# MoE gate and dispatch: tokens laid out as contiguous runs per partition, with large chunks and no transpose

## The chip, the cores and the metric

The kernel runs on one core of a Trainium2 chip. The metric is the device time of one execution in microseconds (us). Before the change it is 252.4 us, the median of 4 runs (252.34 to 252.94). A profiled execution of the same kernel gives the page and the trace; its span, from the first to the last instruction, is 250.4 us.

## What is computed

For each of 16 x 1024 = 16,384 tokens, the two largest of 8 router probabilities are found and normalized to a sum of one. The output holds the token's 512 numbers twice, once for each of the two gates, multiplied by that gate. The lower gate comes first.

```python
x             = randn(16, 1024, 512)   # float32
router_logits = randn(16, 1024, 8)     # float32
k = 2

logits_max = np.max(router_logits, axis=-1, keepdims=True)
probs = np.exp(router_logits - logits_max)
probs = probs / np.sum(probs, axis=-1, keepdims=True)
topk_indices = np.argsort(probs, axis=-1)[..., -k:]
topk_probs = np.take_along_axis(probs, topk_indices, axis=-1)
topk_probs = topk_probs / np.sum(topk_probs, axis=-1, keepdims=True)
x_expanded = x[:, :, np.newaxis, :].repeat(k, axis=2)
return (x_expanded * topk_probs[..., np.newaxis]).astype(np.float32)
```

With k = 2 the normalized gates are the sigmoid of the difference of the two largest logits, and the sigmoid of its negative. The input x is 33.55 MB, the logits are 0.52 MB, and the output is 67.11 MB.

## The kernel before

The 16,384 tokens are seen as 128 tiles of 128 tokens. Token `n*128 + p` lies in tile `n` on partition `p`. One tile of x is 128 rows of 2 KB that lie side by side in memory, and one tile of the output is 128 rows of 4 KB, also side by side.

```python
x_t = x_f.rearrange("(n p) d -> p n d", p=P)
o_t = o_f.rearrange("(n p) d -> p n d", p=P)
rl_A = rl_f.rearrange("(j q) e -> j (q e)", j=P)
...
GRP = 1
NGRP = NT // GRP
xbufs = ctx.enter_context(tc.tile_pool(name="xbufs", bufs=20))
obufs = ctx.enter_context(tc.tile_pool(name="obufs", bufs=8))

logitsA = wpool.tile([P, NT, E], mybir.dt.float32)
nc.sync.dma_start(logitsA, rl_A.rearrange("p (q e) -> p q e", e=E))
```

The logits are loaded in another layout: partition `j` holds those of the 128 neighbouring tokens of tile `j`. On them VectorE finds the two maxima with four wide operations (a maximum, a comparison, a masking, a maximum) and subtracts them. The difference then stands with tiles on partitions, while the scaling needs it with tokens on partitions, so TensorE transposes it through an identity matrix, and ScalarE makes the two sigmoids out of PSUM.

```python
dA = wpool.tile([P, NT], mybir.dt.float32)
nc.vector.tensor_tensor(dA, V[:, :, 0], V[:, :, 1], op=subtract)
dB = psum.tile([P, P], mybir.dt.float32)
nc.tensor.transpose(dB, dA, identity)
nc.scalar.activation(WB[:, 1, :], dB, Sigmoid, scale=1.0)
nc.scalar.activation(WB[:, 0, :], dB, Sigmoid, scale=-1.0)
```

The main loop handles one tile at a time: a load of 256 KB on SyncE's queue, two scalings on VectorE, and a store of 512 KB on ScalarE's queue.

```python
for g in range(NGRP):                       # 128 times
    xg = xbufs.tile([P, GRP, D], f32, tag="xg")
    nc.sync.dma_start(xg, x_t[:, g*GRP:(g+1)*GRP, :])
    og = obufs.tile([P, GRP, K*D], f32, tag="og")
    for slot in range(K):                   # jj loop of one pass left out
        nc.vector.tensor_scalar_mul(
            og[:, 0, slot*D:(slot+1)*D], xg[:, 0, :], WB[:, slot, g:g+1])
    nc.scalar.dma_start(o_t[:, g*GRP:(g+1)*GRP, :], og)
```

There are 20 buffers for tiles of x and 8 for tiles of the output.

Of the kernel before, what the change touches and what calls it, by code (L numbers as in the profile page):

```python
# [1 line left out]

# [5 lines left out]


@with_exitstack
def kernel(
    ctx: ExitStack,
    tc: tile.TileContext,
    x: bass.AP,
    router_logits: bass.AP,
    k: bass.AP,
    out: bass.AP,
):
    nc = tc.nc  # L20
    P = 128

    B, S, D = x.shape
    E = router_logits.shape[-1]
    K = int(k)
    N = B * S

    assert N % P == 0
    NT = N // P
    assert NT == 128, "kernel currently specialised to 16384 tokens"  # L30
    assert E <= 64
    assert 2 <= K <= E

    x_f = x.rearrange("b s d -> (b s) d")
    o_f = out.rearrange("b s k d -> (b s) (k d)")
    rl_f = router_logits.rearrange("b s e -> (b s) e")

    x_t = x_f.rearrange("(n p) d -> p n d", p=P)
    o_t = o_f.rearrange("(n p) d -> p n d", p=P)

    rl_A = rl_f.rearrange("(j q) e -> j (q e)", j=P)

    const = ctx.enter_context(tc.tile_pool(name="const", bufs=1))
    wpool = ctx.enter_context(tc.tile_pool(name="wpool", bufs=1))
    psum = ctx.enter_context(tc.tile_pool(name="psum", bufs=1, space=bass.MemoryType.PSUM))

    GRP = 1
    NGRP = NT // GRP
    xbufs = ctx.enter_context(tc.tile_pool(name="xbufs", bufs=20))
    obufs = ctx.enter_context(tc.tile_pool(name="obufs", bufs=8))  # L50

    logitsA = wpool.tile([P, NT, E], mybir.dt.float32)
    nc.sync.dma_start(logitsA, rl_A.rearrange("p (q e) -> p q e", e=E))  # L53

    identity = const.tile([P, P], mybir.dt.float32)
    make_identity(nc, identity)

    V = wpool.tile([P, NT, K], mybir.dt.float32)
    cur = logitsA
    for i in range(K):  # L60
        nc.vector.reduce_max(  # L61
            V[:, :, i : i + 1], cur, axis=mybir.AxisListType.X
        )
        if i < K - 1:
            eq = wpool.tile([P, NT, E], mybir.dt.float32, tag=f"eq{i}")
            nxt = wpool.tile([P, NT, E], mybir.dt.float32, tag=f"nxt{i}")
            nc.vector.tensor_tensor(  # L67
                eq, cur, V[:, :, i : i + 1].to_broadcast([P, NT, E]),
                op=mybir.AluOpType.is_ge,
            )  # L70
            nc.vector.scalar_tensor_tensor(  # L71
                nxt, eq, -1.0e30, cur,
                op0=mybir.AluOpType.mult, op1=mybir.AluOpType.add,
            )
            cur = nxt

    WB = const.tile([P, K, P], mybir.dt.float32)
    if K == 2:
        dA = wpool.tile([P, NT], mybir.dt.float32)
        nc.vector.tensor_tensor(dA, V[:, :, 0], V[:, :, 1],  # L80
                                op=mybir.AluOpType.subtract)
        dB = psum.tile([P, P], mybir.dt.float32)
        nc.tensor.transpose(dB, dA, identity)  # L83
        nc.scalar.activation(WB[:, 1, :], dB,  # L84
                             mybir.ActivationFunctionType.Sigmoid, scale=1.0)
        nc.scalar.activation(WB[:, 0, :], dB,  # L86
                             mybir.ActivationFunctionType.Sigmoid, scale=-1.0)
    else:
        Em = wpool.tile([P, NT, K], mybir.dt.float32)
        nc.vector.tensor_tensor(  # L90
            Em, V, V[:, :, 0:1].to_broadcast([P, NT, K]),
            op=mybir.AluOpType.subtract,
        )
        nc.scalar.activation(Em, Em, mybir.ActivationFunctionType.Exp)
        Ssum = wpool.tile([P, NT], mybir.dt.float32)
        nc.vector.reduce_sum(Ssum, Em, axis=mybir.AxisListType.X)
        Rinv = wpool.tile([P, NT], mybir.dt.float32)
        nc.vector.reciprocal(Rinv, Ssum)
        W = wpool.tile([P, NT, K], mybir.dt.float32)
        nc.vector.tensor_tensor(  # L100
            W, Em, Rinv.to_broadcast([P, NT, K]), op=mybir.AluOpType.mult
        )
        WB_ps = psum.tile([P, K, P], mybir.dt.float32)
        for slot in range(K):
            nc.tensor.transpose(WB_ps[:, slot, :], W[:, :, K - 1 - slot], identity)
        nc.vector.tensor_copy(WB, WB_ps)

    for g in range(NGRP):
        xg = xbufs.tile([P, GRP, D], mybir.dt.float32, tag="xg")
        nc.sync.dma_start(xg, x_t[:, g * GRP : (g + 1) * GRP, :])  # L110
        og = obufs.tile([P, GRP, K * D], mybir.dt.float32, tag="og")
        for jj in range(GRP):
            j = g * GRP + jj
            for slot in range(K):
                nc.vector.tensor_scalar_mul(  # L115
                    og[:, jj, slot * D : (slot + 1) * D],
                    xg[:, jj, :],
                    WB[:, slot, j : j + 1],
                )
        nc.scalar.dma_start(o_t[:, g * GRP : (g + 1) * GRP, :], og)  # L120


# [1 line left out]
_INS = ['x', 'router_logits', 'k']  # L124
_OUTS = [((16, 1024, 2, 512), 'float32')]
#: Inputs that are plain numbers.
_NUMBERS = {'k': 2}


# [26 lines left out]
```

## Time and profile before

| | before |
|---|---|
| time, median of 4 | 252.4 us |
| span of the profiled execution | 250.4 us |
| bytes moved | 101.26 MB (34.08 read, 67.11 written) |
| mean rate over the span | 404 GB/s |
| VectorE busy | 117.4 us (47%) |
| scaling operations | 256, mean 483 ns |
| loads of x | 128 of 256 KB, median 7.0 us from issue to landing |
| stores | 128 of 512 KB, median 7.5 us from issue to landing |
| first scaling starts | 10.2 us |

In the profile, PE is TensorE's matmul, PEld its weight load, DVE VectorE, ACT ScalarE, POOL GpSimd, SP SyncE; q1 is the DMA queue that SyncE issues to and q10 the one that ScalarE issues to. A row of 40 digits cuts the span in 40 equal slices of 6.3 us, and each digit is the busy share in tenths. The GB/s row has the bytes moved in the same slices. The chain of work that ended last is followed back from the last instruction, and its shares tell which engine or transfer the end hung on. A row of the groups reads: line, engine, operation, output and inputs, shape and count, then busy time in us and mean ns of one, then the idle time of the engine just before these instructions and what ended most of it. A row of the stages reads: the stretch and its length in us; for PE, PEld, DVE, ACT and POOL the busy us and the number of instructions; the granted clock of TensorE; the DMA engines' mean busy share; and GB/s. Shares of DMA can exceed 1 a little where packets of one engine overlap.

### The profile page before, as it was taken

What the parts mean: (1) busy time and instruction counts of PE and PEld (TensorE: products, weight loads), DVE (VectorE), ACT (ScalarE), POOL (GpSimd) and SP (SyncE); (2) the same over time, 40 slices, a digit from 0 to 9 for tenths busy, and PEclk for the clock granted to TensorE, in tenths of its full rate; (3) what the DMA queues carried; (4) which work ended last, traced back from release to release, by engine and by line L of the source; (5) the groups of instructions that cost most, each with busy time, mean ns of one, the idle gap of its engine ahead of it and who ended that gap; (6) DMA issues with size and microseconds to landing.
All of it is one profiled execution on the core that took longest, in us unless ns stands there. A gap on an engine that the chain in (4) does not pass through costs nothing.

```text
span 250.4 us, 932 instructions
## 1 busy us (share of the span) xinstructions
PE 0.4 (0%) x1; PEld 0.2 (0%) x1; DVE 117.4 (47%) x261; ACT 1.7 (1%) x3; POOL 0.7 (0%) x6
## 2 busy tenths in 40 slices
PE   0000000000000000000000000000000000000000
PEld 0000000000000000000000000000000000000000
DVE  3874334344454454454443544544544454467720
ACT  2000000000000000000000000000000000000000
POOL 1000000000000000000000000000000000000000
DMA  7999999999999999999999999999999999999995
GB/s 235 385 411 408 416 410 415 410 418 416 412 417 413 417 414 415 414 417 416 413 417 413 415 416 415 416 415 416 415 414 416 414 415 415 415 419 416 416 414 214
DMA packets 37015, 101.26 MB, mean 404 GB/s; under 512 B 4112, under 2 KB 4112, under 8 KB 37008
## 3 DMA queue, kind: packets, MB, share of 16 engines
q10 hardware_dynamic: 18432, 67.12, 65.6%
q1 hardware_dynamic: 18576, 34.09, 35.7%
q14 instruction: 7, 0.06, 0.1%
HBM read 34.08 MB, written 67.11 MB: 404 GB/s over the span
## 4 chain that ended last, share of the span: by engine, by line
DMA 91%; SPq 2%; DVE 2%; issue 1%; DVEq 0%; ACTq 0%
DMA out_dram<-og 83%; DMA xg<-in_x_dram 8%; SPq L110 2%; DVE og L115 2%; DVEq L151 0%; ACTq L120 0%; SPq L53 0%; DVEq L115 0%
## 5 line engine op out<-in xcount | busy, mean ns | idle before, releaser
L115 DVE TENSOR_SCALAR og<-xg,WB 128x512 f32<-128x512 f32 x256 | 112.2, 483 | 119.0 <-DMA out_dram<-og 78.2
L61 DVE TENSOR_REDUCE V<-logitsA 128x128 f32<-128x1024 f32 x1 | 1.2, 1220 | 3.9 <-DMA logitsA<-in_router_logits_dram 3.9
L84 ACT ACT_TABLE_LOAD x1 | 1.3, 1283 | 0.7 <-PEq L137 0.7
L67 DVE TENSOR_TENSOR eq<-logitsA,V 128x1024 f32<-128x1024 f32 x1 | 1.2, 1226 | 0.0
L71 DVE SCALAR_TENSOR_TENSOR nxt<-eq,logitsA 128x1024 f32<-128x1024 f32 x1 | 1.2, 1224 | 0.0
L61 DVE TENSOR_REDUCE V<-nxt 128x128 f32<-128x1024 f32 x1 | 1.2, 1220 | 0.0
L83 PE MATMUL dB<-identity,dA 128*128 128x128 f32 x1 | 0.4, 446 | 9.4 <-DVE dA L80 9.4
L84 ACT ACTIVATE WB<-dB 128x128 f32<-128x128 f32 x1 | 0.3, 277 | 7.9 <-PE dB L83 7.9
L80 DVE TENSOR_TENSOR dA<-V 128x128 f32<-128x128 f32 x1 | 0.3, 291 | 0.0
masks.py:199 POOL TENSOR_SCALAR_AFFINE_SELECT identity<-identity 128x128 f32<-128x128 f32 x1 | 0.3, 292 | 0.1
L86 ACT ACTIVATE WB<-dB 128x128 f32<-128x128 f32 x1 | 0.3, 272 | 0.0
masks.py:197 POOL MEMSET identity<- 128x128 f32 x1 | 0.2, 204 | 0.3 <-POOLq L137 0.3
L83 PEld LDWEIGHTS dB<-identity,dA 128*128 128x128 f32 x1 | 0.2, 184 | 9.4 <-issue 9.4
L137 POOL MEMSET const-bfloat16-1.0<- 128x1 bf16 x1 | 0.1, 101 | 0.0
L137 POOL MEMSET const-uint8-127<- 128x1 uint8 x1 | 0.1, 101 | 0.0
L137 POOL MEMSET const-float32-0.0<- 128x1 f32 x1 | 0.1, 98 | 0.2 <-issue 0.2
L137 POOL MEMSET const-float32-1.0<- 128x1 f32 x1 | 0.1, 98 | 0.0
## 6 DMA issues: line engine op xcount, KB each, us to landing
out_dram<-og ACTq DMA_DIRECT2D x128, 512.0 KB, 7.5
xg<-in_x_dram SPq DMA_DIRECT2D x128, 256.0 KB, 7.0
logitsA<-in_router_logits_dram SPq DMA_DIRECT2D x1, 512.0 KB, 3.2
```

What stands on the lines that cost most here:

```text
L61: nc.vector.reduce_max(V[:, :, i : i + 1], cur, axis=mybir.AxisListType.X)
L67: nc.vector.tensor_tensor(eq, cur, V[:, :, i : i + 1].to_broadcast([P, NT, E]), op=mybir.AluOpType.is_ge,)
L71: nc.vector.scalar_tensor_tensor(nxt, eq, -1.0e30, cur, op0=mybir.AluOpType.mult, op1=mybir.AluOpType.add,)
L80: nc.vector.tensor_tensor(dA, V[:, :, 0], V[:, :, 1], op=mybir.AluOpType.subtract)
L83: nc.tensor.transpose(dB, dA, identity)
L84: nc.scalar.activation(WB[:, 1, :], dB, mybir.ActivationFunctionType.Sigmoid, scale=1.0)
L86: nc.scalar.activation(WB[:, 0, :], dB, mybir.ActivationFunctionType.Sigmoid, scale=-1.0)
L110: nc.sync.dma_start(xg, x_t[:, g * GRP : (g + 1) * GRP, :])
L115: nc.vector.tensor_scalar_mul(og[:, jj, slot * D : (slot + 1) * D], xg[:, jj, :], WB[:, slot, j : j + 1],)
L137: nc = _bacc.Bacc("TRN2", target_bir_lowering=False, num_devices=1)
```

## The change

Tokens are assigned to partitions the other way round: partition `p` holds the 128 neighbouring tokens `p*128` to `p*128 + 127`. The logits are in this layout already, so the gates come out where the scaling needs them, and the transpose, the identity and PSUM are gone. A load and a store now take 8 tokens of each partition at once: 16 KB runs in x (2 MB in all) and 32 KB runs in the output (4 MB). Between the runs of neighbouring partitions lie 256 KB in x and 512 KB in the output. There are 16 chunks, and 2 buffers for each of x and the output. The first chunk is stored in four parts of 1, 1, 2 and 4 tokens per partition, so that stores begin earlier. The purpose is longer runs in memory, fewer transfers and a shorter way to the gates.

```diff
-    x_t = x_f.rearrange("(n p) d -> p n d", p=P)
-    o_t = o_f.rearrange("(n p) d -> p n d", p=P)
+    x_v = x.rearrange("b s d -> (b s) d").rearrange("(p m) d -> p m d", p=P)
+    o_v = out.rearrange("b s k d -> (b s) (k d)").rearrange(
+        "(p m) d -> p m d", p=P
+    )
...
-    GRP = 1
-    NGRP = NT // GRP
-    xbufs = ctx.enter_context(tc.tile_pool(name="xbufs", bufs=20))
-    obufs = ctx.enter_context(tc.tile_pool(name="obufs", bufs=8))
+    L = 8
+    NCH = M // L
+    xbufs = ctx.enter_context(tc.tile_pool(name="xbufs", bufs=2))
+    obufs = ctx.enter_context(tc.tile_pool(name="obufs", bufs=2))
...
-    identity = const.tile([P, P], mybir.dt.float32)
-    make_identity(nc, identity)
...
-        dB = psum.tile([P, P], mybir.dt.float32)
-        nc.tensor.transpose(dB, dA, identity)
-        nc.scalar.activation(WB[:, 1, :], dB,
-                             mybir.ActivationFunctionType.Sigmoid, scale=1.0)
+        nc.scalar.activation(
+            WA[:, 1, :], dlt, mybir.ActivationFunctionType.Sigmoid, scale=1.0
+        )
...
-    for g in range(NGRP):
-        xg = xbufs.tile([P, GRP, D], mybir.dt.float32, tag="xg")
-        nc.sync.dma_start(xg, x_t[:, g * GRP : (g + 1) * GRP, :])
+    for c in range(NCH):
+        xg = xbufs.tile([P, L, D], mybir.dt.float32, tag="xg")
+        nc.sync.dma_start(xg, x_v[:, c * L : (c + 1) * L, :])
+        og = obufs.tile([P, L, K * D], mybir.dt.float32, tag="og")
+        for l in range(L):
+            m = c * L + l
             for slot in range(K):
                 nc.vector.tensor_scalar_mul(
-                    og[:, jj, slot * D : (slot + 1) * D],
-                    xg[:, jj, :],
-                    WB[:, slot, j : j + 1],
+                    og[:, l, slot * D : (slot + 1) * D],
+                    xg[:, l, :],
+                    WA[:, slot, m : m + 1],
                 )
-        nc.scalar.dma_start(o_t[:, g * GRP : (g + 1) * GRP, :], og)
+            if c == 0 and l in (0, 1, 3):  # first chunk: stores of 1, 1, 2, 4 tokens
+                lo = (0, 1, None, 2)[l]
+                nc.scalar.dma_start(o_v[:, lo : l + 1, :], og[:, lo : l + 1, :])
+        lo = 4 if c == 0 else 0
+        nc.scalar.dma_start(o_v[:, c * L + lo : (c + 1) * L, :], og[:, lo:L, :])
```

More of the change, by code (lines that the diff above doesn't have):

```diff
@@ L6 @@
 from concourse import bass_utils, mybir
-from concourse.masks import make_identity
 from concourse._compat import with_exitstack
@@ L28 @@
     assert N % P == 0
-    NT = N // P
-    assert NT == 128, "kernel currently specialised to 16384 tokens"
+    M = N // P
     assert E <= 64
     assert 2 <= K <= E
-    x_f = x.rearrange("b s d -> (b s) d")
-    o_f = out.rearrange("b s k d -> (b s) (k d)")
-    rl_f = router_logits.rearrange("b s e -> (b s) e")
-    x_t = x_f.rearrange("(n p) d -> p n d", p=P)
-    o_t = o_f.rearrange("(n p) d -> p n d", p=P)
-    rl_A = rl_f.rearrange("(j q) e -> j (q e)", j=P)
-    const = ctx.enter_context(tc.tile_pool(name="const", bufs=1))
@@ L44 @@
-    wpool = ctx.enter_context(tc.tile_pool(name="wpool", bufs=1))
-    psum = ctx.enter_context(tc.tile_pool(name="psum", bufs=1, space=bass.MemoryType.PSUM))
-    GRP = 1
-    NGRP = NT // GRP
-    xbufs = ctx.enter_context(tc.tile_pool(name="xbufs", bufs=20))
-    obufs = ctx.enter_context(tc.tile_pool(name="obufs", bufs=8))
-    logitsA = wpool.tile([P, NT, E], mybir.dt.float32)
-    nc.sync.dma_start(logitsA, rl_A.rearrange("p (q e) -> p q e", e=E))
-    identity = const.tile([P, P], mybir.dt.float32)
@@ L56 @@
-    make_identity(nc, identity)
-    V = wpool.tile([P, NT, K], mybir.dt.float32)
-    cur = logitsA
+    x_v = x.rearrange("b s d -> (b s) d").rearrange("(p m) d -> p m d", p=P)
+    o_v = out.rearrange("b s k d -> (b s) (k d)").rearrange(
+        "(p m) d -> p m d", p=P
+    )
+    rl_v = router_logits.rearrange("b s e -> (b s) e").rearrange(
+        "(p m) e -> p m e", p=P
+    )
+    wpool = ctx.enter_context(tc.tile_pool(name="wpool", bufs=1))
+    L = 8
+    assert M % L == 0
+    NCH = M // L
@@ L60 @@
+    xbufs = ctx.enter_context(tc.tile_pool(name="xbufs", bufs=2))
+    obufs = ctx.enter_context(tc.tile_pool(name="obufs", bufs=2))
+    logits = wpool.tile([P, M, E], mybir.dt.float32)
+    nc.sync.dma_start(logits, rl_v)
+    V = wpool.tile([P, M, K], mybir.dt.float32)
+    cur = logits
     for i in range(K):
-        nc.vector.reduce_max(
-            V[:, :, i : i + 1], cur, axis=mybir.AxisListType.X
-        )
+        nc.vector.reduce_max(V[:, :, i : i + 1], cur, axis=mybir.AxisListType.X)
@@ L64 @@
         if i < K - 1:
-            eq = wpool.tile([P, NT, E], mybir.dt.float32, tag=f"eq{i}")
-            nxt = wpool.tile([P, NT, E], mybir.dt.float32, tag=f"nxt{i}")
+            eq = wpool.tile([P, M, E], mybir.dt.float32, tag=f"eq{i}")
+            nxt = wpool.tile([P, M, E], mybir.dt.float32, tag=f"nxt{i}")
             nc.vector.tensor_tensor(
-                eq, cur, V[:, :, i : i + 1].to_broadcast([P, NT, E]),
+                eq, cur, V[:, :, i : i + 1].to_broadcast([P, M, E]),
                 op=mybir.AluOpType.is_ge,
@@ L75 @@
             cur = nxt
-    WB = const.tile([P, K, P], mybir.dt.float32)
+    WA = wpool.tile([P, K, M], mybir.dt.float32)
     if K == 2:
-        dA = wpool.tile([P, NT], mybir.dt.float32)
-        nc.vector.tensor_tensor(dA, V[:, :, 0], V[:, :, 1],
-                                op=mybir.AluOpType.subtract)
-        dB = psum.tile([P, P], mybir.dt.float32)
-        nc.tensor.transpose(dB, dA, identity)
-        nc.scalar.activation(WB[:, 1, :], dB,
-                             mybir.ActivationFunctionType.Sigmoid, scale=1.0)
-        nc.scalar.activation(WB[:, 0, :], dB,
-                             mybir.ActivationFunctionType.Sigmoid, scale=-1.0)
+        dlt = wpool.tile([P, M], mybir.dt.float32)
+        nc.vector.tensor_tensor(
+            dlt, V[:, :, 0], V[:, :, 1], op=mybir.AluOpType.subtract
+        )
+        nc.scalar.activation(
+            WA[:, 1, :], dlt, mybir.ActivationFunctionType.Sigmoid, scale=1.0
+        )
+        nc.scalar.activation(
+            WA[:, 0, :], dlt, mybir.ActivationFunctionType.Sigmoid, scale=-1.0
+        )
     else:
-        Em = wpool.tile([P, NT, K], mybir.dt.float32)
+        Em = wpool.tile([P, M, K], mybir.dt.float32)
         nc.vector.tensor_tensor(
-            Em, V, V[:, :, 0:1].to_broadcast([P, NT, K]),
+            Em, V, V[:, :, 0:1].to_broadcast([P, M, K]),
             op=mybir.AluOpType.subtract,
@@ L94 @@
         nc.scalar.activation(Em, Em, mybir.ActivationFunctionType.Exp)
-        Ssum = wpool.tile([P, NT], mybir.dt.float32)
+        Ssum = wpool.tile([P, M], mybir.dt.float32)
         nc.vector.reduce_sum(Ssum, Em, axis=mybir.AxisListType.X)
-        Rinv = wpool.tile([P, NT], mybir.dt.float32)
+        Rinv = wpool.tile([P, M], mybir.dt.float32)
         nc.vector.reciprocal(Rinv, Ssum)
[L99 to L103, printed above, removed]
-        for slot in range(K):
-            nc.tensor.transpose(WB_ps[:, slot, :], W[:, :, K - 1 - slot], identity)
-        nc.vector.tensor_copy(WB, WB_ps)
-    for g in range(NGRP):
-        xg = xbufs.tile([P, GRP, D], mybir.dt.float32, tag="xg")
-        nc.sync.dma_start(xg, x_t[:, g * GRP : (g + 1) * GRP, :])
-        og = obufs.tile([P, GRP, K * D], mybir.dt.float32, tag="og")
-        for jj in range(GRP):
-            j = g * GRP + jj
+        for slot in range(K):
+            nc.vector.tensor_tensor(
+                WA[:, slot, :],
+                Em[:, :, K - 1 - slot],
+                Rinv,
+                op=mybir.AluOpType.mult,
+            )
+    for c in range(NCH):
[4 more added lines that the diff above has]
+            m = c * L + l
             for slot in range(K):
                 nc.vector.tensor_scalar_mul(
-                    og[:, jj, slot * D : (slot + 1) * D],
-                    xg[:, jj, :],
-                    WB[:, slot, j : j + 1],
-                )
-        nc.scalar.dma_start(o_t[:, g * GRP : (g + 1) * GRP, :], og)
+                    og[:, l, slot * D : (slot + 1) * D],
+                    xg[:, l, :],
+                    WA[:, slot, m : m + 1],
+                )
+            if c == 0 and l in (0, 1, 3):
[3 more added lines that the diff above has]
+        nc.scalar.dma_start(o_v[:, c * L + lo : (c + 1) * L, :], og[:, lo:L, :])
 _INS = ['x', 'router_logits', 'k']
```

## The prediction

> **What bounds the kernel now.** I read the page from the top: first the busy times, then the 40 slices, then the queues, the chain, and last the trace cut into stages. The first two say which resource is full.
>
> ```profile
> PE 0.4 (0%) x1; PEld 0.2 (0%) x1; DVE 117.4 (47%) x261; ACT 1.7 (1%) x3; POOL 0.7 (0%) x6
> ...
> DMA  7999999999999999999999999999999999999995
> GB/s 235 385 411 408 416 410 415 410 418 416 412 417 413 417 414 415 414 417 416 413 417 413 415 416 415 416 415 416 415 414 416 414 415 415 415 419 416 416 414 214
> ```
>
> No engine is more than half busy; the DMA row is 9 in every slice but the first and last, and the bytes flow at 410 to 419 GB/s from slice 3 to slice 39. The chain agrees: it is nearly all transfers, and VectorE's own work is 2% of it.
>
> ```profile
> DMA 91%; SPq 2%; DVE 2%; issue 1%; DVEq 0%; ACTq 0%
> ...
> L115 DVE TENSOR_SCALAR og<-xg,WB 128x512 f32<-128x512 f32 x256 | 112.2, 483 | 119.0 <-DMA out_dram<-og 78.2
> ```
>
> VectorE's 119.0 us of idle time before the scaling line is mostly a wait for a store to give its buffer back (78.2 us). That is how a DMA-bound loop looks from the engine, and removing engine work can't shorten it. So the span is bytes over rate, plus a start and an end. The stages give these two:
>
> ```profile
> 0.00:2.00 2.00, 0.00 (x0) 0.00 (x0) 0.00 (x0) 1.27 (x1) 0.70 (x6) 1.00 0.14 41
> ...
> 4.00:6.00 2.00, 0.00 (x0) 0.00 (x0) 1.97 (x2) 0.00 (x0) 0.00 (x0) 1.00 0.93 285
> ...
> 8.00:10.00 2.00, 0.45 (x1) 0.18 (x1) 1.23 (x2) 0.11 (x1) 0.00 (x0) 1.00 1.04 396
> ...
> 100.00:200.00 100.00, 0.00 (x0) 0.00 (x0) 45.88 (x104) 0.00 (x0) 0.00 (x0) 1.00 1.04 415
> ...
> 240.00:244.00 4.00, 0.00 (x0) 0.00 (x0) 0.46 (x2) 0.00 (x0) 0.00 (x0) 1.00 1.03 415
> ```
>
> The last two columns are the DMA engines' busy share and GB/s. 101.26 MB at 415 GB/s are 244.0 us. The span is 250.4 us, so 6.4 us lie outside the plateau: about 2.0 us until bytes flow, about 1.5 us lost to slow transfers between 2 and 9 us, and about 2.9 us from the last full-rate stretch (near 247.5 us) to the end. The reported time is 2.0 us above the span (252.4 against 250.4).
>
> The queue lines show in what pieces the bytes move:
>
> ```profile
> DMA packets 37015, 101.26 MB, mean 404 GB/s; under 512 B 4112, under 2 KB 4112, under 8 KB 37008
> ...
> q10 hardware_dynamic: 18432, 67.12, 65.6%
> q1 hardware_dynamic: 18576, 34.09, 35.7%
> ```
>
> 18,432 packets over 128 stores are 144 each: 128 of data, one row of 4 KB per partition, and 16 short ones, one per DMA engine. The loads have the same count with 2 KB rows. So every piece is 2 or 4 KB.
>
> **What the Trainium skill says.** Three places, all in "DMA: Bandwidth & Descriptors". (1) "Where 436 GB/s comes from": 16 ports give a ceiling of 435 GB/s. The plateau of 415 is 95% of that; no run so far shows 435. (2) "Why small descriptors are slow (HBM only)": every packet carries a fixed overhead of a few cycles, so larger pieces lose less; "Measured" on the same page has 425 GB/s for a 16 MB load. The trace fits an overhead: in steady state (60 to 200 us) the store queue held 67.6% of 16 engines and moved 38.71 MB, the load queue held 35.9% and moved 19.33 MB. Per data packet, with its share of the short ones, that is 0.160 us for 4 KB and 0.085 us for 2 KB. The shares add up to 1.036, because packets overlap, so I divide by that: 154.6 and 82.2 ns. The second 2 KB cost 72.4 ns, so some 10 ns of each packet don't depend on its size. (3) "Latency and other measured facts", the row on HBM row pitch: copies with a pitch of 512 KiB between partitions ran at 207 GB/s per direction against 214 when padded, larger powers of two at far less. No trace here shows such a pitch yet: before, the 128 rows of a transfer lie side by side.
>
> **The change part by part.**
>
> *Gates.* The transpose goes: matmul 0.45 us, its hand-over to ScalarE, and the identity on GpSimd, which was never on the path. The four wide VectorE operations (1.2 us each) and the subtract stay. Before, the gates were ready at about 10.2 us; without PE they could be ready at about 9.8. But the first x chunk is now 2.10 MB and VectorE needs all of it. The trace before had moved about 2.9 MB by 10 us, and logits plus chunk 0 are 2.62 MB, so with completion the chunk arrives at about 10 to 11 us. The 0.4 us are hidden. Gain: 0.
>
> *VectorE.* 256 scalings at 483 ns stay: 16 of them, 7.7 us, for each of 16 chunks. A chunk moves 2.10 MB in and 4.19 MB out, 14 to 15 us of transfer. When a chunk's scaling starts, a 4.19 MB store has just been queued or is still running, about 10 us of work, so DMA stays fed with only two buffers of each kind. Cost in steady state: 0, but the margin is about 2 us against issue and completion times.
>
> *Start.* Loads queued ahead shrink from 20 tiles (5.2 MB) to two chunks (4.2 MB), which last until about 13 to 14 us. Stores then start with one token of every partition (0.52 MB), at about 11 us issued and 12.5 us flowing, and follow at the rate of VectorE: 0.52 MB per 0.97 us. The fourth store of the first chunk (2.1 MB) must wait for four tokens, 3.9 us, while the 1.05 MB before it last only 2.5 us; load 2 also comes only when chunk 0 is finished. I put 1.0 us of idle DMA here.
>
> *End.* The last chunk is scaled in 7.7 us beside the store of the one before (9.8 us at 430 GB/s), which just covers it with issue and completion. I put 0.5 us.
>
> *Rate.* This is where any gain must come from. A load now has 16 KB runs per partition and a store 32 KB (4 to 16 KB in the first chunk), and there are 36 transfers instead of 257. If a run moves as one piece, the overhead of 10 ns per piece nearly vanishes: 72.4 ns per 2 KB alone would be 453 GB/s, above the skill's ceiling, so the ceiling would bind: about 432 GB/s. If the hardware cuts runs into pieces of 4 KB, loads and stores both look like the stores of before: 154.6 ns for 4 KB, 424 GB/s at most; but the store-only end of the trace, all 4 KB rows, shows just 415, so I say 416 to 421. If the pitch costs something (512 KiB between output rows, 256 KiB between input rows) the 3% of the skill's row would take 432 to about 419.
>
> *Sum.* Fixed parts: 6.4 us as before, plus 1.5 us, is 7.9 us; plus 2.0 us from span to time. With 432 GB/s: 234.4 + 7.9 + 2.0 = 244.3 us. With 428: 236.6 + 9.9 = 246.5 us. With 420: 241.1 + 9.9 = 251.0 us. With 415: 253.9 us.
>
> **The rivals.**
>
> *A: long runs, ceiling reached (430 to 434 GB/s), 243 to 246 us.* For it: the fixed part per packet in the trace, and that the logits transfer already moves a merged 4 KB run per partition although its view has rows of 32 bytes (18,576 packets on q1 are 129 transfers of 144). Against: store-only stages don't exceed 420 now.
>
> *B: the plateau isn't set by packets but by HBM, or runs are cut up; 415 to 422 GB/s, 250 to 254 us.* For it: the store-only end (4 KB) runs at 415, the mixture of 2 and 4 KB at 415 too, and loads of 2 KB alone at 396 to 410 around 10 us. If packet size were everything, the stores alone ought to be visibly faster than the mixture. Then only the 1.5 us of new idle time would be seen.
>
> *C: the pitch collides.* All 16 engines write at addresses that differ by multiples of 512 KiB; if that costs 5% or more, the rate falls to 395 to 405, 260 to 266 us. Against it: the skill's figure at 512 KiB is only 3% low, [...]and a third of the bytes has half the pitch.
>
> *D: two buffers are too few.* If issue plus completion takes over 2 us on top of 7.7 us, DMA idles in each of 14 chunks by perhaps 0.5 us: 7 us, which would eat A's gain. Against it: a load and a store are queued together, so there are usually two transfers outstanding.
>
> **Range and chances.** I take A as somewhat likelier than B, and lean the point to 428 GB/s: 246.5 us. Faster by 2% means under 247.4 us, a rate of at least 426.5 GB/s: 0.47. Within 2% (247.4 to 257.4 us) is B, or A spoiled by D or a mild C: 0.41. Slower is C or a bad D: 0.12. The range of 241.5 to 253.0 us holds A and most of B.
>
> **What would show it.** If A is right, the packet list has data packets over 8 KB (128 per transfer, some 4,100 in all), and plateau slices near 430 GB/s with a DMA share of 9. Packets still under 8 KB, some 25,000 of them, with 416 to 422 GB/s, mean B. A busy share of 9 with under 410 GB/s means C. Slices with a share of 7 or 8, and VectorE waiting while the queues are short, mean D. The start is right if the first scaling begins at 10 to 11 us; the end, if full rate holds to about 3 us before the end. I am wrong outright if the plateau leaves 395 to 434 GB/s, or if start and end lose over 5 us more than before.

## The result and the profile after

The changed kernel takes 242.66 us in the median (before, in runs beside it: 252.53 us). The ratio is 0.9621, with a 95% interval of 0.9598 to 0.9644: 3.8% faster. The prediction had said 246.5 us, in a range of 241.5 to 253.0.

The first lines are from the changed kernel's page: busy times, packets, queues, the chain by engine, and the group of the scaling line.

```profile
DVE 107.9 (44%) x261; ACT 1.8 (1%) x3; POOL 0.2 (0%) x4
...
DMA packets 5186, 101.21 MB, mean 415 GB/s; under 512 B 576, under 2 KB 576, under 8 KB 960
...
q10 hardware_dynamic: 2736, 67.11, 65.7%
q1 hardware_dynamic: 2448, 34.08, 33.0%
...
DMA 68%; DVE 26%; issue 0%; DVEq 0%; ACT 0%
...
L106 DVE TENSOR_SCALAR og<-xg,WA 128x512 f32<-128x512 f32 x256 | 102.7, 481 | 118.3 <-DMA out_dram<-og 118.0
```

The bytes are the same, but 5,186 packets carry them where 37,015 did. On q10, 19 stores of 128 rows and 16 short packets each make the 2,736: so a run of 32 KB goes as one packet and is not cut. VectorE still waits for stores (118.0 us), so the kernel is still bound by DMA. The 26% of the chain on VectorE are no new bound: a chunk's scaling must end before its store can start, but other transfers run beside it (the DMA row below is 9 in every slice but the first and last).

That execution was a disturbed one (span 244.1 us; the ratios leave such runs out, the medians do not), so the rates are read from a second profile of the same kernel, with a span of 240.1 us. Its 40 slices:

```profile
DMA  6999999999999999999999999999999999999995
GB/s 262 437 401 426 434 431 445 434 408 404 456 437 412 439 431 439 420 423 461 404 442 445 418 439 431 433 423 426 458 420 426 439 428 418 423 461 415 437 437 235
```

And its stages; the columns are as before, without PE and PEld, as TensorE does nothing now:

```profile
4.00:6.00 2.00, 1.54 (x2) 0.00 (x0) 0.00 (x0) 1.00 0.94 401
...
12.00:14.00 2.00, 2.00 (x6) 0.00 (x0) 0.00 (x0) 1.00 0.88 336
...
60.00:200.00 140.00, 63.53 (x159) 0.00 (x0) 0.00 (x0) 1.00 1.01 432
...
215.00:220.00 5.00, 0.00 (x0) 0.00 (x0) 0.00 (x0) 1.00 0.95 410
```

The engines were full before (share 1.04) and are full now (1.01), yet they move 432 GB/s instead of 415. The slices swing more, from 404 to 461 in the steady part, presumably because a packet of 16 or 32 KB is counted in one lump; the 401 of the third slice is a real dip (the row for 12 to 14 us). 101.21 MB at 432 GB/s are 234.3 us against 244.0 us, 9.7 us less. What lies outside the plateau is 5.8 us (240.1 - 234.3) against 6.4 us. Both together are the 10.3 us between the spans.

### The profile page after: what moved, and what is told of

Its sections match the earlier page's. It is cut to its first block, busy times and chain, and to the rows that moved or that the text cites. A ratio compares the mean times of both kernels' runs of the same rounds, so it can differ in the third digit from the quotient of the medians.

```text
span 244.1 us, 392 instructions
## 1 busy us (share of the span) xinstructions
DVE 107.9 (44%) x261; ACT 1.8 (1%) x3; POOL 0.2 (0%) x4
## 2 busy tenths in 40 slices
DMA packets 5186, 101.21 MB, mean 415 GB/s; under 512 B 576, under 2 KB 576, under 8 KB 960
## 3 DMA queue, kind: packets, MB, share of 16 engines
q10 hardware_dynamic: 2736, 67.11, 65.7%
## 4 chain that ended last, share of the span: by engine, by line
DMA 68%; DVE 26%; issue 0%; DVEq 0%; ACT 0%
DMA out_dram<-og 66%; DVE og L106 24%; DMA logits<-in_router_logits_dram 1%; DVE V L54 1%; DVE eq L58 1%; DVE nxt L62 1%; DVEq L146 0%; DVEq L106 0%; ACT WA L74 0%; DVE dlt L71 0%
## 5 line engine op out<-in xcount | busy, mean ns | idle before, releaser
L106 DVE TENSOR_SCALAR og<-xg,WA 128x512 f32<-128x512 f32 x256 | 102.7, 481 | 118.3 <-DMA out_dram<-og 118.0
L54 DVE TENSOR_REDUCE V<-logits 128x128 f32<-128x1024 f32 x1 | 1.2, 1220 | 4.0 <-DMA logits<-in_router_logits_dram 4.0
L58 DVE TENSOR_TENSOR eq<-logits,V 128x1024 f32<-128x1024 f32 x1 | 1.2, 1226 | 0.0
L62 DVE SCALAR_TENSOR_TENSOR nxt<-eq,logits 128x1024 f32<-128x1024 f32 x1 | 1.2, 1224 | 0.0
L74 ACT ACTIVATE WA<-dlt 128x128 f32<-128x128 f32 x1 | 0.3, 310 | 7.4 <-DVE dlt L71 7.4
L77 ACT ACTIVATE WA<-dlt 128x128 f32<-128x128 f32 x1 | 0.3, 293 | 0.0
```

Source lines behind the costliest of these rows:

```text
L54: nc.vector.reduce_max(V[:, :, i : i + 1], cur, axis=mybir.AxisListType.X)
L58: nc.vector.tensor_tensor(eq, cur, V[:, :, i : i + 1].to_broadcast([P, M, E]), op=mybir.AluOpType.is_ge,)
L62: nc.vector.scalar_tensor_tensor(nxt, eq, -1.0e30, cur, op0=mybir.AluOpType.mult, op1=mybir.AluOpType.add,)
L74: nc.scalar.activation(WA[:, 1, :], dlt, mybir.ActivationFunctionType.Sigmoid, scale=1.0)
L77: nc.scalar.activation(WA[:, 0, :], dlt, mybir.ActivationFunctionType.Sigmoid, scale=-1.0)
L106: nc.vector.tensor_scalar_mul(og[:, l, slot * D : (slot + 1) * D], xg[:, l, :], WA[:, slot, m : m + 1],)
```

## The experiments

The theory is that the length of a contiguous run sets the rate: a run goes as one piece (one packet), and each piece has a fixed cost. Its rivals: the number of transfers (257 to 36), the way to the gates without a transpose, and, as something that takes away part of the gain, the pitch of 256 and 512 KiB and having only two buffers. All times are medians, and all ratios are to the kernel before, run beside them on the same chip.

### Same transfers, short pieces

```diff
-        xg = xbufs.tile([P, L, D], mybir.dt.float32, tag="xg")
-        nc.sync.dma_start(xg, x_v[:, c * L : (c + 1) * L, :])
+        xg = xbufs.tile([P, L, D + 8], mybir.dt.float32, tag="xg")
+        nc.sync.dma_start(xg[:, :, 0:D], x_v[:, c * L : (c + 1) * L, :])
# the output tile likewise: K * D + 8, and [..., 0 : K * D] in its stores
```

> The changed kernel with each token's row in SBUF padded by 32 bytes in both the x and the output tiles, so that the same 36 transfers of the same bytes at the same addresses in memory are cut into pieces of 2 KB (x) and 4 KB (output). Theory of piece size (a fixed cost of about 10 ns per piece): the gain vanishes, 250 to 253 us, some 25,000 data packets, plateau 412 to 417 GB/s. Theory of transfer count (257 to 36 transfers, so fewer semaphore packets and hand-overs): the gain stays, 242 to 244 us.

Measured: 251.7 us, ratio 0.9974 (0.996 to 0.9988). Packets, a plateau stage and a stage near the end:

```profile
DMA packets 33475, 101.21 MB, mean 403 GB/s; under 512 B 577, under 2 KB 577, under 8 KB 33473
...
60.00:200.00 140.00, 57.82 (x144) 0.00 (x0) 0.00 (x0) 1.00 1.03 417
...
235.00:240.00 5.00, 3.31 (x9) 0.00 (x0) 0.00 (x0) 1.00 0.59 242
```

The number of transfers, the addresses in memory, the buffers and the gates are those of the changed kernel; only the pieces are short, and the plateau falls to 417 GB/s and with it nearly all of the gain. The transfer count is out as the main cause, and so is the order of the rows in memory, which the padding in SBUF leaves as it is. The last row shows a loss that the changed kernel does not have: DMA at 0.59 for 5 us, about 2 us. The last chunk's load lands only at 231.9 us, and the store before it runs out while the chunk is scaled.

### One token per transfer, in the new layout

```diff
-    L = 8
+    L = 1
-    xbufs = ctx.enter_context(tc.tile_pool(name="xbufs", bufs=2))
-    obufs = ctx.enter_context(tc.tile_pool(name="obufs", bufs=2))
+    xbufs = ctx.enter_context(tc.tile_pool(name="xbufs", bufs=20))
+    obufs = ctx.enter_context(tc.tile_pool(name="obufs", bufs=8))
# and no split of the first chunk's stores
```

> The changed layout and its gates without a transpose, but one token of each partition per transfer (256 transfers, pieces of 2 and 4 KB, 20 and 8 buffers as in the kernel before). Piece size: 251 to 253 us, as before. If the shorter way to the gates were worth something by itself: 1 us or more below the kernel before, under 251.5 us. If the pitch of 256 and 512 KiB between partitions costs rate: above 255 us.

Measured: 252.91 us, ratio 1.0014 (1.0005 to 1.0024); its steady stage:

```profile
60.00:200.00 140.00, 64.29 (x147) 0.00 (x0) 0.00 (x0) 1.00 1.04 415
```

The layout and the gates without TensorE are worth nothing by themselves, and the pitch costs nothing with short pieces: the same 415 GB/s as before, where the rows of a transfer lay side by side.

### Long runs side by side, no pitch

```diff
-    x_v = x.rearrange("b s d -> (b s) d").rearrange("(p m) d -> p m d", p=P)
+    x_v = x.rearrange("b s d -> (b s) d").rearrange("(c p l) d -> c p l d", p=P, l=8)
# the output and the logits likewise; a load takes x_v[c], a store o_v[c, :, ...]
```

> Runs of 16 and 32 KB as in the changed kernel, but the runs of neighbouring partitions lie side by side in memory, so a chunk is one contiguous 2 MB or 4 MB region and there is no pitch of 256 or 512 KiB; the logits come in runs of 256 bytes instead of 4 KB. If the pitch costs nothing: 242 to 244 us, the logits landing up to 1 us later. If the pitch costs 2% or more of the rate: 237 to 240 us, plateau above 430 GB/s.

Measured: 244.38 us, ratio 0.9656 (0.9622 to 0.9689). Stages:

```profile
20.00:24.00 4.00, 4.00 (x11) 0.00 (x0) 0.00 (x0) 1.00 0.87 328
...
60.00:200.00 140.00, 63.69 (x159) 0.00 (x0) 0.00 (x0) 1.00 1.00 432
...
225.00:235.00 10.00, 4.62 (x12) 0.00 (x0) 0.00 (x0) 1.00 0.90 387
```

The time is 0.4 us above the range for "the pitch costs nothing", while a plateau above 430 GB/s was the sign put down for the opposite: the first profile of the changed kernel has 423 GB/s from 100 to 200 us. The second profile decides it: the changed kernel also holds 432 GB/s, so the pitch costs nothing with long pieces either. What this kernel loses, it loses at the ends: the logits land at 5.2 us instead of 4.4 (they come in runs of 256 bytes), the first stores come later, and DMA is short of work at 20 to 24 us and again at 225 to 235 us.

### The old layout in large transfers

```diff
-    GRP = 1
+    GRP = 8
-    xbufs = ctx.enter_context(tc.tile_pool(name="xbufs", bufs=20))
-    obufs = ctx.enter_context(tc.tile_pool(name="obufs", bufs=8))
+    xbufs = ctx.enter_context(tc.tile_pool(name="xbufs", bufs=2))
+    obufs = ctx.enter_context(tc.tile_pool(name="obufs", bufs=2))
```

> The kernel before with 8 tiles per transfer (its own GRP = 8) and 2 buffers each: 32 large transfers, but pieces of 2 and 4 KB. Transfer count: 243 to 247 us. Piece size: no gain in the plateau (412 to 417 GB/s), and since the first store now waits for 16 scalings, some 3 to 6 us lost at the start: 254 to 258 us.

Measured: 256.88 us, ratio 1.0167 (1.0152 to 1.0183). Stages (with PE and PEld again):

```profile
16.00:20.00 4.00, 0.00 (x0) 0.00 (x0) 4.00 (x11) 0.00 (x0) 0.00 (x0) 1.00 0.29 27
...
60.00:200.00 140.00, 0.00 (x0) 0.00 (x0) 57.82 (x144) 0.00 (x0) 0.00 (x0) 1.00 1.03 417
```

Transfers of 2 and 4 MB with pieces of 2 and 4 KB run at 417 GB/s. The first row shows what the split of the first chunk is for: without it DMA stands nearly still for 4 us, while VectorE fills a whole chunk. (The changed kernel without its split was not run.) So large transfers of short rows, with two buffers and no split, are 4.3 us slower than the kernel before: what they lose at the start is more than the 2 GB/s that the plateau gains.

### Two and four tokens per transfer

As the run with one token, with `L = 2` (10 and 8 buffers) and `L = 4` (5 and 4 buffers).

> The changed kernel with 2 tokens of each partition per transfer: pieces of 4 and 8 KB, 10 and 8 buffers, all stores of one size. From the runs with short pieces (417 GB/s, 16 pieces for 48 KB of each DMA engine) and with long ones lying side by side (432 GB/s, 2.25 pieces): 65 ns over 14 pieces, 4.6 ns a piece. With 9 pieces: about 424 GB/s and 246 to 248 us. If only runs of over 8 KB were faster (a threshold): 250 us or more.

> As the run with two tokens, with 4: pieces of 8 and 16 KB, 5 and 4 buffers. By 4.6 ns a piece, with 4.5 pieces: about 429 GB/s and 243.5 to 245.5 us. If the changed kernel gained from something other than piece length, such as the split first chunk, it would stay above 247 us.

Measured: 246.87 us, ratio 0.9767 (0.9749 to 0.9785), and 243.2 us, ratio 0.9623 (0.9605 to 0.9641). The page and the steady stage of two tokens:

```profile
DMA packets 18581, 101.24 MB, mean 413 GB/s; under 512 B 2064, under 2 KB 2064, under 8 KB 10384
...
60.00:200.00 140.00, 62.01 (x149) 0.00 (x0) 0.00 (x0) 1.00 1.02 425
```

And of four:

```profile
DMA packets 9363, 101.22 MB, mean 420 GB/s; under 512 B 1040, under 2 KB 1040, under 8 KB 1168
...
60.00:200.00 140.00, 61.91 (x152) 0.00 (x0) 0.00 (x0) 1.00 1.01 429
```

Two tokens came as foretold; four were 0.3 us below the range, at the plateau foretold. Outside the plateau they lose 5.2 us (241.1 - 235.9), against 5.8 in the changed kernel, and the dip at 12 to 14 us is missing (438 GB/s). There is no threshold: the rate climbs with each doubling. That gives a line. One token of every partition is 48 KB for each of the 16 engines (128 x 6 KB / 16), so 786,432 bytes over the plateau's rate is the time of 48 KB, and the page's packets over 2,048 (16 engines, 128 tokens) are the pieces in it:

| kernel | pieces per 48 KB | plateau, GB/s | ns per 48 KB |
|---|---|---|---|
| before | 18.1 | 415 | 1895 |
| short pieces | 16.3 | 417 | 1886 |
| two tokens | 9.1 | 425 | 1850 |
| four tokens | 4.6 | 429 | 1833 |
| changed kernel | 2.5 | 432 | 1820 |

From the first row to the last: 75 ns over 15.5 pieces are 4.8 ns a piece (rates read to 1 GB/s leave about 0.3 either way), and at no pieces 1808 ns remain, 435 GB/s. The three rows between lie within 3 ns of this line.

### The changed kernel once more

The kernel is unchanged.

> The changed kernel once more, beside the others on the same chip: 242 to 243.5 us, plateau 426 to 432 GB/s. If its layout with a pitch costs rate against the chunks lying side by side (432 GB/s): 424 GB/s or less.

Measured: 242.3 us, ratio 0.9588 (0.9567 to 0.9609), plateau 432 GB/s, as shown above, and the same as with the runs side by side. The pitch is no cost.

### More buffers

Only the buffer counts of the changed kernel are edited:

```diff
-    xbufs = ctx.enter_context(tc.tile_pool(name="xbufs", bufs=2))
-    obufs = ctx.enter_context(tc.tile_pool(name="obufs", bufs=2))
+    xbufs = ctx.enter_context(tc.tile_pool(name="xbufs", bufs=4))
+    obufs = ctx.enter_context(tc.tile_pool(name="obufs", bufs=3))
```

> The changed kernel with 4 buffers for x and 3 for the output instead of 2 and 2. If two buffers starve the DMA only at the start (loads run out at about 12 us while the first stores are small) and before the last chunk: 0.5 to 2 us less than the changed kernel, 240.5 to 242 us, with the stretch from 12 to 14 us near full rate. If two buffers starve it in every chunk: 3 us or more less, under 239.5 us, and a higher plateau. If they are enough everywhere: 242.7 us as before.

Measured: 248.66 us, ratio 0.9847 (0.9822 to 0.9872): a miss, and in the other direction. Stages:

```profile
12.00:14.00 2.00, 2.00 (x6) 0.00 (x0) 0.00 (x0) 1.00 1.02 401
...
60.00:200.00 140.00, 60.71 (x152) 0.00 (x0) 0.00 (x0) 1.00 1.00 427
...
238.00:240.00 2.00, 0.00 (x0) 0.00 (x0) 0.00 (x0) 1.00 0.38 164
240.00:242.00 2.00, 0.00 (x0) 0.00 (x0) 0.00 (x0) 1.00 0.15 66
242.00:244.00 2.00, 0.00 (x0) 0.00 (x0) 0.00 (x0) 1.00 0.08 33
```

The dip at 12 to 14 us did close. But the plateau is 1% lower, and the end is ragged for 6 us, where the kernel before takes 2 us (shares of 0.31 and 0.09 from 247 to 249 us): a share of 0.08 is about one engine of 16 still at work while the others have finished. I took it that some engines had fallen behind. Four more runs asked what lets them.

> The changed kernel with 4 buffers for x and 2 for the output. More buffers (4 and 3) cost 6 us, and the rate fell off raggedly over the last 9 us. Theory of drift: spare buffers let some of the 16 DMA engines run ahead of others, and the end waits for the last one; what matters is how far stores, two thirds of the bytes, can run ahead, so with 2 output buffers 241.5 to 244 us and a short end. Theory of load order: early loads take the place of stores, and that alone costs; then 246 to 249 us here too.

> The changed kernel with 2 buffers for x and 3 for the output. Drift: 245 to 249 us with a ragged end. Load order: 241.5 to 243.5 us, since loads can't run ahead.

> The chunks lying side by side in memory (no pitch), with 4 and 3 buffers. If the drift comes from the pitch of 256 and 512 KiB (some engines meeting slower memory): no ragged end, 241 to 243 us. If DMA engines drift apart whatever the addresses: 247 to 250 us.

> The changed kernel with 3 buffers for x and 2 for the output: a candidate for the best version, as the third load fills the dip at 12 to 14 us, where the loads queued ahead had run out (336 GB/s there). Drift theory with stores as the driver: 241.3 to 242.3 us, up to 1 us below the changed kernel. Load order: 243.5 to 246 us.

| buffers for x / output | time, us | ratio (95%) |
|---|---|---|
| 2 / 2 | 242.3 | 0.9588 (0.9567 to 0.9609) |
| 2 / 3 | 242.64 | 0.9598 (0.9575 to 0.9621) |
| 3 / 2 | 244.98 | 0.9672 (0.9623 to 0.972) |
| 4 / 2 | 247.28 | 0.98 (0.9747 to 0.9854) |
| 4 / 3 | 248.66 | 0.9847 (0.9822 to 0.9872) |
| 4 / 3, runs side by side | 252.3 (in the ratio: 248.8, 250.6) | 0.9883 (0.9842 to 0.9924) |

My theory that stores running ahead pull the engines apart failed in three runs of three: a third output buffer changes nothing (though one of the four executions took 247.45 us), and four x buffers cost some 5 us. Three x buffers lie between, but scatter (243.1 to 247.9 us), and their interval overlaps the first comparison's 0.9598 to 0.9644 for two: that they cost time is likely, not shown. The rival, early loads, met its ranges in all three. With the runs side by side the loss is there too (0.9883, against 0.9656 with two buffers each), so it does not need the pitch; the four executions scatter from 248.8 to 257.6 us, and the two that the ratio counts lie in and just above the range of 247 to 250. Traffic in the first 30 us shows what x buffers do (packets, MB, share of 16 engines). With 4 and 2 buffers:

```profile
q1 hardware_dynamic: 800, 10.22, 82.7%
q10 hardware_dynamic: 337, 1.45, 11.7%
```

With 2 and 2:

```profile
q1 hardware_dynamic: 592, 7.08, 57.7%
q10 hardware_dynamic: 591, 4.69, 37.1%
```

3.1 MB of loads went ahead of 3.2 MB of stores. No bytes were added, and the price appears late. With 4 and 2 buffers (the profiled execution, 249.71 us, is the slowest of its four):

```profile
60.00:140.00 80.00, 33.26 (x83) 0.00 (x0) 0.00 (x0) 1.00 1.01 425
140.00:200.00 60.00, 25.36 (x64) 0.00 (x0) 0.00 (x0) 1.00 1.00 414
200.00:215.00 15.00, 6.76 (x17) 0.00 (x0) 0.00 (x0) 1.00 0.82 352
```

From 200 to 215 us DMA stands partly idle, while VectorE waits for stores to end. I read this as engines that have done their part of the stores they were given while others haven't. The traces bear out that engines fall behind: each transfer ends in 16 short packets, taken here as one per engine. In the changed kernel's second profile the first and the last of a store's 16 start 0.4 us apart at first and never more than 1.7 us (4.3 in the first profile, whose rate is lower too); with 2 and 3 buffers, never more than 1.9 us. With 4 and 2 the distance grows from 0.4 us to 6.8 us, and with 4 and 3 from 1.5 to 8.9 us; with the runs side by side it reaches 7.9 us. Why loads that are further ahead make engines uneven stays open, and no run removed it. No buffer count tried beats 2 and 2.

## Why the prediction was right

**Runs go as one piece, and the rate rises to the ceiling: right.** I had put 432 GB/s where long runs aren't cut, and the plateau is 432. Rival A asked for some 4,100 packets over 8 KB; the page has 4,226 (5,186 less the 960 under 8 KB; runs of 8 KB and more). Short pieces in the same transfers take nearly all of the gain away.

**The cost of a piece: right in kind, twice too large.** I took 10 ns from the packets' own durations, scaled for their overlap; the line through five plateaus gives 4.8 ns. The line rests on rates, so it is the better measure; that the overlap (shares that add up to 1.036) misled me is likely, but not shown. It did no harm, because 10 ns would have led beyond the ceiling and I cut it there. The Trainium skill, "DMA: Bandwidth & Descriptors", "Why small descriptors are slow (HBM only)", speaks of about 3 cycles per packet; if they are cycles of the 850 MHz fabric of "Where 436 GB/s comes from", which the page doesn't say, an estimate is 3.5 ns, below the measured 4.8 but of its order. The line's 435 GB/s at no pieces is also that section's ceiling.

**Leaning to 428 GB/s: too cautious, 2.3 us.** 101.26 MB at 428 GB/s are 236.6 us, and the plateau made them 234.3. I leaned because stores alone at 4 KB ran at 415 like the mixture (rival B). With 9 packets for 32 KB at 4.8 ns the line gives about 420 for stores alone, so even under A they would have been only 5 GB/s faster, little to go by in a stretch of 4 us. Why they ran at 415 the line does not explain. Rival B fell with the long runs, of two and four tokens and of eight. The range held both A and most of B, and even no change at all, so that it came true says little. What came true is A, and 242.66 us lies just below A's own 243 to 246, as the fixed parts were put too large.

**The fixed parts: 7.9 us put, 5.8 measured, 2.1 us.** I kept 1.5 us for the slow transfers between 2 and 9 us and added 1.5 us. The slow stretch mostly went away: 401 GB/s at 4 to 6 us, where it was 285. The dip where the loads run out came where I had it (12 to 14 us, 336 GB/s), but costs (432 - 336) / 432 x 2 = 0.4 us, not 1.0. The dip near the end is (432 - 410) / 432 x 5 = 0.3 us, not 0.5. These two terms, 2.3 and 2.1 us, bring 246.5 to 242.1 us; the profiled execution of the second profile took 241.93.

**The gates: a small step that was wrong.** I had said that the first x chunk would come later than the gates, at 10 to 11 us. The changed kernel's timeline (start, length, then the wait in brackets) says otherwise:

```profile
9.38 0.31 ACT L74 ACTIVATE WA<-dlt 128x128 f32<-128x128 f32 x1 [7.38 <-DVE dlt L71]
9.60 0.29 ACT L77 ACTIVATE WA<-dlt 128x128 f32<-128x128 f32 x1
9.72 12.76 DVE L106 TENSOR_SCALAR og<-xg,WA 128x512 f32<-128x512 f32 x32 [0.38 <-ACT WA L74]
...
30.64 6.42 DVE L106 TENSOR_SCALAR og<-xg,WA 128x512 f32<-128x512 f32 x16 [8.16 <-DMA out_dram<-og]
```

The scaling waited for the gates, so the chunk was already there. (In the second profile it waited for them too, until 10.12 us.) From the landing of the logits to the first scaling it is now 5.7 us (4.03 to 9.72), where it was 6.25 (3.95 to 10.20): 0.6 us shorter. That it is worth nothing was right: the run with one token has it too (4.35 to 10.05), and is not faster.

**A chunk's scaling: too long.** I had put 7.7 us for 16 scalings, 16 times the mean of one. The last row above has 6.42 us: scalings overlap, as 256 of 481 ns fill only 102.7 us of busy time. Stores are ready sooner than I had reckoned, which fits the two small dips; no run tests that alone. A smaller slip: the slices of the kernel before run from 408, not 410, to 419 GB/s.

**Rival C, the pitch: out.** With pitch and without, long runs give 432 GB/s, short ones 415 to 417. The 3% in the skill's section "Latency and other measured facts" is for copies within HBM and doesn't show here, where one side of each transfer is SBUF. **Rival D, two buffers: out:** a third output buffer gains nothing, and four load buffers are worse.

## What to carry to other kernels

When DMA is the bound and its engines are full, count the packets: over rows of 2 to 32 KB, longer contiguous runs per partition gave rate (415 to 432 GB/s) and larger transfers of short rows gave next to none (417). Lay the tokens out so that a partition's share of a chunk is one run in memory and in SBUF; a few bytes of padding between rows in SBUF undo it. See that the first stores are small, so that DMA has work while the first chunk is computed: by a split, or by smaller chunks as with four tokens. Try fewer load buffers as well as more: here 4.2 MB of loads ahead were enough, and 8.4 MB cost time.

## What the runs showed that I had not expected

Spare load buffers slowed this kernel, which DMA bounds: with 4 buffers of 2 MB in place of 2 the time rose from 242.3 to 247.3 us (with 3, less surely, to 245.0), with a plateau of 425 and later 414 GB/s in place of 432. The engines came apart by up to 6.8 us within one store, where it is 1.7 us with 2. A third store buffer of 4 MB made no difference (242.64 us). Five load buffers of 1 MB, with four tokens per transfer, did no harm (429 GB/s, 1.8 us), so the number of buffers alone is not it. What pulls the engines apart is not settled.

A rate that depends on piece length so regularly, 4.8 ns a piece from 2 KB to 32 KB with 435 GB/s at no pieces, was not expected either.
